# Token-major products of a two-layer hybrid backbone: one pass over the weights for two token tiles

## The chip, the cores and the metric

The kernel runs as one program on one core of a Trainium2 chip. A core has a matrix engine (TensorE, PE), a vector engine (VectorE, DVE), a scalar engine (ScalarE, ACT), GpSimd (POOL), a queue engine (SyncE, SP) that issues the DMAs, and 16 DMA engines. Matrix products are written to PSUM, which has eight banks of 512 fp32 columns on 128 partitions; everything else lies in SBUF. The metric is the device time of one execution in microseconds (us). Before the change the median of three runs is 2991.73 us (2989.30 to 2992.11).

## The reference

Two layers over 256 latent tokens and 256 context tokens of width 1024, in fp32. Each layer is a half-step SwiGLU, a parallel token mixing and a second half-step SwiGLU, all with adaptive shift, scale and gate. The token mixing starts from one wide input projection of the normalised tokens:

```
cols_x = split_cols(hx @ p['w_in'], IN_SPLITS)     # latent tokens
cols_s = split_cols(hs @ p['w_in'], IN_SPLITS)     # context tokens
# IN_SPLITS: retention q, k, v, gate; attention q, k, v; RWKV inputs; three branch gates
ret_x = retention_output(ox_f + flip_seq(ox_b), cols_x[3])
att_x = merge_att_heads(window_context_attention(aqx, akx, avx, aks, avs, sink), hx.dtype)
rwkv_x = rwkv_output(yx_f + yx_b, r_x, v_x, dirs_x, g_x, p)
out_x = branch_merge(ret_x, att_x, rwkv_x, cols_x[8], p)
```

Retention runs over 8 heads of 64 keys and 128 values, attention over 8 query and 2 key heads of 64 with a norm and a rotary step on queries and keys, RWKV-7 over 8 heads of 64 as a recurrence in both directions. In the second layer only the latent tokens have outputs; the context tokens still give keys, values and final states.

## The kernel before

Activations lie feature-major: 8 tiles of 128 features by 512 tokens (columns 0 to 255 context, 256 to 511 latent). Each such tile is held as a high and a low part (`hall`), and so is each weight, and a product takes three matmuls per slice of the contraction: high by high, high by low, low by high. That is `mm3`, lines 186 to 188, which nearly all products go through.

Weights come in one stream per stage, packed in the order of use in tiles of four 128x128 blocks (`PB = 4`, 256 KB). `Weights.get` (lines 104 to 121) hands out a block. When the tile that it lies in is not held, it issues the DMA (`raw`), an ACT copy to the high part (`whi`, L114) and a DVE subtract to the low part (`wlo`, L115), and then keeps this tile and the one just before it, no others. There are 8 buffers of `raw`, 4 of `whi` and 3 of `wlo`.

Most products (`dense`) have the weights stationary and the tokens moving, 512 or 256 columns, so that the result is feature-major. Three kinds need tokens on partitions instead: the retention values (`ret_proj`, four head pairs per layer, 256 columns each), the attention keys and values (`att_kv`, once per layer) and the attention queries (`att_q`, two groups of 256 columns per layer). There the tokens are stationary, 128 at a time, and the weights move, 256 columns. Each product covers 16 blocks: 8 slices of the contraction by two blocks side by side. In layer 0 these lie in 4 tiles; in layer 1 the stream is shifted by two blocks, and they touch 5. A half (256 tokens) is computed as two token tiles into the two halves of one bank (`ps_mm`, two buffers); the first tile's whole contraction runs before the second's:

```
for t in range(2):
    tk = slice(half * 256 + t * 128, half * 256 + t * 128 + 128)
    for kt in range(KT):
        mm3(o[:, t * 256:t * 256 + 256], hl(H[kt], tk), W.get(bl[2 * kt], 2), kt == 0, kt == KT - 1)
```

Since only two tiles are held, the walk over the weights is fetched, cast and subtracted anew for each token tile: four walks per product where both halves are wanted, two in `att_q` of layer 1. What reads the bank (a mean in `ret_proj`, the norm in `qk_norm`) reads both token tiles together.

The order of the work in the mixing stage is the string `ORDER[l]`: `P` retention projections of a head pair, `H` one retention head, `kv`, `q` and `t` attention, `c` the RWKV columns of a head pair, `A`/`C` the front steps of its context and latent halves (`rw_prep`), `B`/`D` their merge and recurrence (`rw_back`), `G` gates. From this stream a scheduler makes one fixed order of instructions for each engine, which moves an instruction past others on its engine where its own timing model finds it ready. On the chip each engine follows its order strictly. A front step ends in matmuls of L973; POOL then solves 32x32 triangles for every head and chunk (L1001, L1002), the result goes through a DRAM tile (`td`) back to SBUF (`z`), and the merge begins with stream transposes on DVE (L1016, L1020) and 32x32 matmuls on PE (L1028). The recurrence follows (L1070 to L1101).

Of the kernel before, what the change touches and what calls it, by code (L numbers as in the profile page):

```python
# [20 lines left out]
KT = 8  # L21
# [101 lines left out]
def body(nc, tc, I, O, es, dbg=None):  # L123
# [10 lines left out]
    def ps(tag):  # L134
        return pp.tile([128, 512], F32, name="ps_" + tag, tag=tag, bufs=NB[tag])
# [49 lines left out]
    def mm3(o, w, h, start, stop):  # L185
        PE.matmul(o, w[0], h[0], start=start, stop=False)  # L186
        PE.matmul(o, w[0], h[1], start=False, stop=False)  # L187
        PE.matmul(o, w[1], h[0], start=False, stop=stop)  # L188
# [138 lines left out]
    def hl(h, c):  # L327
        return h[0][:, c], h[1][:, c]
# [151 lines left out]
    def ret_decay(h, st):  # L480
# [12 lines left out]
        V.tensor_tensor(dt[1], dt[1], e, ALU.add)  # L493
        return dt

    def ret_proj(W, H, p, S, st):
        c = span(S)
        full = slice(0, 512)
        o = ps("mm")
        dense(W, f"rq{p}", H, c, o)  # L500
        q = rope_fm(o, c, st)
        o = ps("mm")
        dense(W, f"rk{p}", H, full, o)
        k = rope_fm(o, full, st)
        bl = W.take(f"rv{p}")
        v = []
        for half in range(2):
            o = ps("mm")
            for t in range(2):
                tk = slice(half * 256 + t * 128, half * 256 + t * 128 + 128)  # L510
                for kt in range(KT):
                    mm3(o[:, t * 256:t * 256 + 256], hl(H[kt], tk), W.get(bl[2 * kt], 2), kt == 0, kt == KT - 1)
            ov = o.rearrange("p (a d) -> p a d", d=128)
            mu = sm(4, "mu")
            V.tensor_reduce(mu, ov, axis=AX.X, op=ALU.add)
            V.tensor_scalar(mu, mu, -1.0 / 1024, None, ALU.mult)
            vt = ft()
            V.scalar_tensor_tensor(vt.rearrange("p (a d) -> p a d", d=128), ov, 0.125, mu.unsqueeze(2).to_broadcast([128, 4, 128]), ALU.mult, ALU.add)
            v.append(vt)
        st["ret"] = q, k, v  # L520
# [131 lines left out]
        st["aeye"] = ph[:, 0:64].bitcast(BF16)  # L652
        A.copy(st["aeye"], ident)

    def att_tok(W, H, bl, half):
        o = ps("mm")
        for t in range(2):
            tk = slice(half * 256 + t * 128, half * 256 + t * 128 + 128)
            for kt in range(KT):
                mm3(o[:, t * 256:t * 256 + 256], hl(H[kt], tk), W.get(bl[2 * kt], 2), kt == 0, kt == KT - 1)  # L660
        return o

    def qk_norm(o, nh, half, j, st):

        nc_ = nh * 64
# [37 lines left out]
    def att_kv(W, H, st):  # L703
        bl = W.take("akv")
        kt_ = ps("ap")
        vt = mk([128, 512], "kv", 1)
        for half in range(2):
            o = att_tok(W, H, bl, half)
            z = qk_norm(o, 2, half, 1, st)
            for t in range(2):  # L710
                q = half * 2 + t
                PE.transpose(kt_[:, q * 128:q * 128 + 128], z[:, t * 256:t * 256 + 128], ident)
                A.copy(vt[:, q * 128:q * 128 + 128], o[:, t * 256 + 128:t * 256 + 256])
        kd = [mk([128, 512], "kd", 2, F32R) for h in range(2)]
        kl = [mk([128, 512], "kl", 2, F32R) for h in range(2)]
        for h in range(2):
            hs, ot = (slice(64 * x, 64 * x + 64) for x in (h, 1 - h))
            A.copy(kd[h][hs], kt_[hs])
            A.copy(kd[h][ot], kt_[hs])
            V.tensor_sub(kl[h][hs], kt_[hs], kd[h][hs].bitcast(F32))  # L720
            V.tensor_sub(kl[h][ot], kt_[hs], kd[h][hs].bitcast(F32))
        st["kT"], st["v"] = (kd, kl), vt

    def att_q(W, H, grp_, S, st):
        bl = W.take(f"aq{grp_}")
        c = span(S)
        qT = [[mk([128, 512], "qT", 4, F32R) for h in range(2)] for pr in range(2)]
        for half in S:
            o = att_tok(W, H, bl, half)
            z = qk_norm(o, 4, half, 0, st)  # L730
            pt = ps("ap")
            for pr in range(2):
                for t in range(2):
                    PE.transpose(pt[:, pr * 256 + t * 128:pr * 256 + t * 128 + 128], z[:, t * 256 + pr * 128:t * 256 + pr * 128 + 128], ident)
            for pr in range(2):
                for h in range(2):
                    hs, ot = (slice(64 * x, 64 * x + 64) for x in (h, 1 - h))
                    A.copy(qT[pr][h][hs, CS[half]], pt[hs, pr * 256:pr * 256 + 256])
                    V.tensor_sub(qT[pr][h][ot, CS[half]], pt[hs, pr * 256:pr * 256 + 256], qT[pr][h][hs, CS[half]].bitcast(F32))
        st["qT", 2 * grp_], st["qT", 2 * grp_ + 1] = qT  # L740
# [474 lines left out]
    for l in range(2):  # L1215
# [5 lines left out]
        if l == 0:  # L1221
# [3 lines left out]
            H = norm(0, 0, 0, both, fine)  # L1225
            tk = tasks(0, range(2, 9))
        else:
            H = norm(1, 0, 0, both)
            ada_cond()
            tk = tasks(1, range(5, 9))  # L1230
        W = Weights(nc, mk, I[f"w{l}a"], plan_ffn("f1i", "f1o"))
# [4 lines left out]
        H = norm(l, 1, 3, both)  # L1236
# [3 lines left out]
        W = Weights(nc, mk, I[f"w{l}b"], plan_mix(l), True)  # L1240
# [114 lines left out]
```

## Time and profile before

| | |
|---|---|
| median of three runs | 2991.73 us (2989.30 to 2992.11) |
| the profiled execution | 2988.53 us, span from first to last instruction 2986.8 us |
| granted clock of TensorE, mean | 0.962 |
| PE busy | 2847.7 us (95%) |
| DVE busy | 2061.5 us (69%) |
| ACT busy | 1324.0 us (44%) |
| POOL busy | 388.8 us (13%) |
| read from HBM | 398.74 MB |

The layers' mixing stages stand at about 400 to 1330 us and 2090 to 2790 us of the span; before, between and behind them are the SwiGLU steps. A row of the views names the line, the engine, the operation and its tiles (output<-inputs) by the program's names: `ps_mm<-hall,whi` is a product with weights stationary, `ps_mm<-whi,hall` and `ps_mm<-wlo,hall` one with tokens stationary. A matmul's row lasts from its issue to its modelled end, and the rows of a running product overlap.

### The profile page before, as it was taken

How to read it: one execution, taken by the hardware profiler on the slowest of the kernel's cores; microseconds unless marked ns; L12 is line 12 of the kernel's file. 1: busy time of each engine (PE TensorE's matmuls, PEld its weight loads, DVE VectorE, ACT ScalarE, POOL GpSimd, SP SyncE). 2: the span in 40 equal slices, each digit the busy share in tenths (PEclk: the TensorE clock that was granted, in tenths of full speed). 3: DMA queues.
4: the chain of work that ended last, by engine and by line, in shares of the span. 5: the costliest groups of instructions: out<-in, count | busy, mean ns of one | idle time of the engine just before them, and what ended most of it. 6: DMA issues, size and time to landing. Idle time of an engine off the chain costs nothing.

```text
span 2986.8 us, 48345 instructions
## 1 busy us (share of the span) xinstructions
PE 2847.7 (95%) x17081; PEld 2427.4 (81%) x17081; DVE 2061.5 (69%) x4677; ACT 1324.0 (44%) x2892; POOL 388.8 (13%) x1068
## 2 busy tenths in 40 slices
PE   8999998899989999999999999999989999989999
PEld 7888887777877787788888888888778888779999
DVE  7977679785685665667756476455887778668655
ACT  3222245554454554333223332233666565655544
POOL 0000002432032121000000000000033434230000
PEclk9999999887999999999999999999989899999999
DMA  7756445332343144543544435343444344257563
GB/s 271 234 177 201 148 131 163 102 97 60 101 141 101 58 147 134 174 171 136 193 140 148 145 110 194 103 162 118 136 138 134 102 136 122 72 166 228 177 191 115
DMA packets 276434, 431.43 MB, mean 144 GB/s; under 512 B 80608, under 2 KB 98144, under 8 KB 276192
## 3 DMA queue, kind: packets, MB, share of 16 engines
q1 hardware_dynamic: 276192, 428.35, 44.8%
q8 instruction: 134, 2.20, 0.3%
q14 instruction: 108, 0.88, 0.1%
HBM read 398.74 MB, written 25.82 MB: 142 GB/s over the span
## 4 chain that ended last, share of the span: by engine, by line
PE 77%; DVE 7%; POOL 6%; DMA 4%; issue 2%; ACT 2%; SPq 1%; POOLq 0%; DVEq 0%; ACTq 0%
PE ps_mm L187 20%; PE ps_mm L188 20%; PE ps_mm L186 20%; POOL cst L1002 3%; POOL cst L1001 3%; PE ps_rf L973 2%; PE ps_mm L364 1%; DVE wlo L115 1%; PE ps_po L776 1%; DMA z<-td 1%; PE ps_po L553 1%; PE ps_rx L1077 1%; PE ps_rx L1070 1%; PE ps_rx L364 1%; PE ps_rx L1045 1%
## 5 line engine op out<-in xcount | busy, mean ns | idle before, releaser
L114 ACT CAST whi<-raw 128x512 fp32r<-128x512 f32 x1070 | 629.4, 617 | 700.3 <-PE ps_mm L187 372.7
L188 PE MATMUL ps_mm<-hall,wlo 128*128 128x512 f32 (+1 forms) x2320 | 845.0, 365 | 2.8 <-DVE wlo L115 2.7
L186 PE MATMUL ps_mm<-hall,whi 128*128 128x512 f32 (+1 forms) x2320 | 843.5, 364 | 3.5 <-ACT ft L583 2.5
L187 PE MATMUL ps_mm<-hall,whi 128*128 128x512 f32 (+1 forms) x2320 | 840.0, 362 | 0.0
L115 DVE TENSOR_TENSOR wlo<-raw,whi 128x512 fp32r<-128x512 f32 x1070 | 720.4, 690 | 87.7 <-ACT whi L114 72.9
L186 PEld LDWEIGHTS ps_mm<-hall,whi 128*128 128x128 f32 x2320 | 443.2, 191 | 74.1 <-ACT ft L583 2.7
L188 PEld LDWEIGHTS ps_mm<-hall,wlo 128*128 128x128 f32 x2320 | 442.1, 191 | 73.8 <-DVE wlo L115 4.2
L187 PEld LDWEIGHTS ps_mm<-hall,whi 128*128 128x128 f32 x2320 | 442.2, 191 | 73.3 <-issue 0.7
L186 PE MATMUL ps_mm<-hid,whi 128*128 128x512 f32 (+1 forms) x737 | 260.6, 354 | 0.0
L187 PE MATMUL ps_mm<-hid,whi 128*128 128x512 f32 (+1 forms) x737 | 260.0, 354 | 0.0
L188 PE MATMUL ps_mm<-hid,wlo 128*128 128x512 f32 (+1 forms) x737 | 257.3, 354 | 0.0
L1001 POOL TENSOR_TENSOR cst<-acc,cst 128x60 f32<-128x60 f32 (+24 forms) x496 | 176.5, 356 | 571.9 <-DMA acc<-ad__11190 55.8
L401 DVE TENSOR_TENSOR ft<-ft,ps_mm 128x512 f32<-128x512 f32 (+1 forms) x80 | 49.7, 622 | 211.4 <-PE ps_mm L188 198.3
L373 DVE SCALAR_TENSOR_TENSOR x<-ps_mm,cst,x 128x256 f32<-128x256 f32 x136 | 61.0, 480 | 192.2 <-PE ps_mm L188 192.1
L853 POOL TENSOR_TENSOR ll<-lora,lh 128x512 fp32r<-128x512 f32 x8 | 10.7, 1338 | 1396.6 <-DVE cst L199 954.4
L1002 POOL TENSOR_TENSOR cst<-cst 128x60 f32<-128x60 f32 (+24 forms) x496 | 183.0, 369 | 37.9
L236 DVE SCALAR_TENSOR_TENSOR ft<-m,cd 128x1024 bf16<-128x1024 f32 x136 | 162.8, 1219 | 7.0 <-DMA m<-ada 6.9
L237 DVE SCALAR_TENSOR_TENSOR m<-m,cd 128x1024 f32<-128x1024 f32 x136 | 165.2, 1220 | 0.7
L187 PEld LDWEIGHTS ps_mm<-hid,whi 128*128 128x128 f32 x737 | 139.0, 189 | 19.6
L186 PEld LDWEIGHTS ps_mm<-hid,whi 128*128 128x128 f32 x737 | 139.0, 189 | 19.6
L188 PEld LDWEIGHTS ps_mm<-hid,wlo 128*128 128x128 f32 x737 | 138.4, 189 | 19.2
L187 PE MATMUL ps_mm<-wlo,hall 128*128 128x256 f32 x416 | 134.0, 323 | 19.9 <-DVE wlo L115 19.1
(338 smaller groups left out, 4493.4 us busy)
## 6 DMA issues: line engine op xcount, KB each, us to landing
m<-ada SPq DMA_DIRECT2D x136, 512.0 KB, 4.5
raw<-w1b SPq DMA_DIRECT2D x271, 256.0 KB, 3.9
raw<-w0b SPq DMA_DIRECT2D x270, 256.0 KB, 3.2
raw<-w0a SPq DMA_DIRECT2D x132, 256.0 KB, 2.8
raw<-w0c SPq DMA_DIRECT2D x132, 256.0 KB, 4.8
raw<-w1a SPq DMA_DIRECT2D x132, 256.0 KB, 4.1
raw<-w1c SPq DMA_DIRECT2D x132, 256.0 KB, 3.0
gd<-ft SPq DMA_DIRECT2D x24, 256.0 KB, 2.0
```

What stands on the lines that cost most here:

```text
L114: nc.scalar.copy(hi, raw)
L115: nc.vector.tensor_sub(lo, raw, hi.bitcast(F32))
L186: PE.matmul(o, w[0], h[0], start=start, stop=False)
L187: PE.matmul(o, w[0], h[1], start=False, stop=False)
L188: PE.matmul(o, w[1], h[0], start=False, stop=stop)
L236: V.scalar_tensor_tensor(junk, raw, 1.0, st["cond"][0], ALU.mult, ALU.mult, accum_out=md[:, kt, 0:1])
L237: V.scalar_tensor_tensor(raw, raw, 1.0, st["cond"][1], ALU.mult, ALU.mult, accum_out=md[:, kt, 1:2])
L364: PE.matmul(o[:, p], w[k, j][q], hl(H[k], p)[0], start=(k == 0 and q == 0 and p.start == c.start), stop=False)
L373: V.scalar_tensor_tensor(xs[n][:, CS[s]], o[:, CS[s]], gate[:, n, s:s + 1], xs[n][:, CS[s]], ALU.mult, ALU.add)
L973: PE.matmul(ov[:, q, 0:n], kb[d][hs, q].rearrange("p a t -> p (a t)"), ar[d][hs, q].rearrange("p a t -> p (a t)")[:, 0:n], start=True, sto ...
L1001: G.tensor_tensor(w, acc[j // 16][:, j % 16, j + 1:32].unsqueeze(1).to_broadcast([128, m, n]), tt[:, 0:m, j:j + 1].to_broadcast([128, m, n ...
L1002: G.tensor_tensor(tt[:, 0:m, j + 1:32], tt[:, 0:m, j + 1:32], w, ALU.add)
```

## The change

One helper takes the place of the loop in `ret_proj` and of `att_tok`. The slices of the contraction are outside and the two token tiles inside, so a pair of weight blocks is asked for once and serves both tiles. The start flag is set for the first matmul on the bank alone, and the stop flag for the last.

```
+    def tokens(W, H, bl, half):
+
+        o = ps("mm")
+        for kt in range(KT):
+            w = W.get(bl[2 * kt], 2)
+            for t in range(2):
+                tk = slice(half * 256 + t * 128, half * 256 + t * 128 + 128)
+                mm3(o[:, t * 256:t * 256 + 256], hl(H[kt], tk), w, kt == 0 and t == 0, kt == KT - 1 and t == 1)
+        return o
+
     def ret_proj(W, H, p, S, st):
...
         for half in range(2):
-            o = ps("mm")
-            for t in range(2):
-                tk = slice(half * 256 + t * 128, half * 256 + t * 128 + 128)
-                for kt in range(KT):
-                    mm3(o[:, t * 256:t * 256 + 256], hl(H[kt], tk), W.get(bl[2 * kt], 2), kt == 0, kt == KT - 1)
+            o = tokens(W, H, bl, half)
...
-    def att_tok(W, H, bl, half):
-        o = ps("mm")
-        for t in range(2):
-            tk = slice(half * 256 + t * 128, half * 256 + t * 128 + 128)
-            for kt in range(KT):
-                mm3(o[:, t * 256:t * 256 + 256], hl(H[kt], tk), W.get(bl[2 * kt], 2), kt == 0, kt == KT - 1)
-        return o
-
...
-            o = att_tok(W, H, bl, half)
+            o = tokens(W, H, bl, half)
```

The two kernels' orders hold the same instructions but for 116 weight tiles: 116 rows of L114 on ACT, of L115 on DVE and of the `raw` DMA on SP are not in the changed one. Lines of the RWKV part have numbers lower by 2 after the change (L1028 is L1026), those of the retention heads higher by 6 (L515 is L521).

PE in the first group of token products of layer 0 (names with their numbers, so that a weight tile can be told from the next), before:

```order
L186 MATMUL ps_mm_4631<-whi_4645,hall_66 128x256
L187 MATMUL ps_mm_4631<-wlo_4646,hall_66 128x256
L188 MATMUL ps_mm_4631<-whi_4645,hall_66 128x256
L186 MATMUL ps_mm_4631<-whi_4645,hall_66 128x256
L187 MATMUL ps_mm_4631<-wlo_4646,hall_66 128x256
L188 MATMUL ps_mm_4631<-whi_4645,hall_66 128x256
L186 MATMUL ps_mm_4631<-whi_4657,hall_66 128x256
L187 MATMUL ps_mm_4631<-wlo_4658,hall_66 128x256
L188 MATMUL ps_mm_4631<-whi_4657,hall_66 128x256
```

and after the change:

```order
L186 MATMUL ps_mm_4607<-whi_4645,hall_66 128x256
L187 MATMUL ps_mm_4607<-wlo_4646,hall_66 128x256
L188 MATMUL ps_mm_4607<-whi_4645,hall_66 128x256
L186 MATMUL ps_mm_4607<-whi_4645,hall_66 128x256
L187 MATMUL ps_mm_4607<-wlo_4646,hall_66 128x256
L188 MATMUL ps_mm_4607<-whi_4645,hall_66 128x256
L186 MATMUL ps_mm_4607<-whi_4645,hall_66 128x256
L187 MATMUL ps_mm_4607<-wlo_4646,hall_66 128x256
L188 MATMUL ps_mm_4607<-whi_4645,hall_66 128x256
L186 MATMUL ps_mm_4607<-whi_4645,hall_66 128x256
L187 MATMUL ps_mm_4607<-wlo_4646,hall_66 128x256
L188 MATMUL ps_mm_4607<-whi_4645,hall_66 128x256
```

A pair of weight tiles (high and low) serves 6 matmuls before and 12 after.

DVE in the last retention-value product of layer 1, between the reading of its first half and that of its second (L515, after the change L521, is the mean over a half), before:

```order
L515 TENSOR_REDUCE cst<-ps_mm 128x4
L115 TENSOR_TENSOR wlo<-raw,whi 128x512 x2
L516 TENSOR_SCALAR cst<-cst 128x4
L115 TENSOR_TENSOR wlo<-raw,whi 128x512
L518 SCALAR_TENSOR_TENSOR ft<-ps_mm,cst 128x512
L115 TENSOR_TENSOR wlo<-raw,whi 128x512 x7
L515 TENSOR_REDUCE cst<-ps_mm 128x4
```

and after the change, from the same row on:

```order
L521 TENSOR_REDUCE cst<-ps_mm 128x4
L115 TENSOR_TENSOR wlo<-raw,whi 128x512
L537 TENSOR_TENSOR rks<-ft,rks 64x512
L1099 TENSOR_TENSOR rb<-rb,ps_rx 64x128
L1018 STREAM_TRANSPOSE tg<-z 32x8x32
L115 TENSOR_TENSOR wlo<-raw,whi 128x512
L1018 STREAM_TRANSPOSE tg<-z 32x8x32
L522 TENSOR_SCALAR cst<-cst 128x4
L980 STREAM_TRANSPOSE rt<-rt 64x256
L976 TENSOR_TENSOR gk<-ps_rf,cst 64x512
L978 TENSOR_TENSOR tg<-ps_rf,cst 64x256
L115 TENSOR_TENSOR wlo<-raw,whi 128x512
```

Ten low parts stood there and five stand now, and steps of the RWKV chain, with the transposes of the solve's result among them, have moved in between.

PE at the merge of the context half of the last head pair in layer 1, before:

```order
L186 MATMUL ps_mm<-whi,hall 128x256
L187 MATMUL ps_mm<-wlo,hall 128x256
L188 MATMUL ps_mm<-whi,hall 128x256
L186 MATMUL ps_mm<-whi,hall 128x256
L1028 MATMUL ps_rx<-rb,cst 32x32 x8
L1028 MATMUL ps_rx<-z,cst 32x32
L187 MATMUL ps_mm<-wlo,hall 128x256
```

and after the change:

```order
L186 MATMUL ps_mm<-hall,whi 128x256
L1123 MATMUL ps_rx<-cst,rb 128x64 x4
L1124 MATMUL ps_rx<-lo,cst 128x256
L1026 MATMUL ps_rx<-rb,cst 32x32 x8
L1026 MATMUL ps_rx<-z,cst 32x32 x8
L187 MATMUL ps_mm<-hall,whi 128x256
```

The merge has moved from within the last token product to a later product with the weights stationary. Between this merge and the next one, that of the latent half, stand 261 rows of PE's order before and 130 after.

## Rows read from the trace of the kernel before

**Rows 1.** The page, part 1: busy us (share of the span) xinstructions.

```profile
PE 2847.7 (95%) x17081; PEld 2427.4 (81%) x17081; DVE 2061.5 (69%) x4677; ACT 1324.0 (44%) x2892; POOL 388.8 (13%) x1068
```

**Rows 2.** Timeline of PE inside a token product: start us, us, instruction.

```profile
461.60 0.28 PE L186 MATMUL ps_mm<-whi,hall 128*128 128x256 f32 x1
461.71 0.28 PE L187 MATMUL ps_mm<-wlo,hall 128*128 128x256 f32 x1
...
462.54 0.28 PE L188 MATMUL ps_mm<-whi,hall 128*128 128x256 f32 x1
```

**Rows 3.** Groups by line: xcount | busy us, mean ns | idle before <-releasers.

```profile
L115 DVE TENSOR_TENSOR wlo<-raw,whi 128x512 fp32r<-128x512 f32 x1069 | 720.0, 691 | 87.7 <-ACT whi L114 72.9 <-PE ps_mm L188 5.7 <-POOL cst L1001 2.7
L114 ACT CAST whi<-raw 128x512 fp32r<-128x512 f32 x1069 | 629.1, 617 | 700.3 <-PE ps_mm L187 372.7 <-issue 272.7 <-PE ps_mm L188 16.6
...
L187 PE MATMUL ps_mm<-wlo,hall 128*128 128x256 f32 x416 | 134.0, 323 | 19.9 <-DVE wlo L115 19.1
L186 PE MATMUL ps_mm<-whi,hall 128*128 128x256 f32 x416 | 122.0, 296 | 2.5 <-ACT whi L114 0.9 <-DVE ft L518 0.8 <-DVE ft L572 0.7
L188 PE MATMUL ps_mm<-whi,hall 128*128 128x256 f32 x416 | 121.5, 293 | 0.0
```

**Rows 4.** Windows: us, busy of PE, PEld, DVE, ACT, POOL, clock, DMA share, GB/s.

```profile
459.00:500.00 41.00, 34.05 (x254) 30.77 (x252) 40.40 (x86) 28.08 (x59) 2.07 (x5) 1.00 0.67 207
818.00:842.00 24.00, 23.38 (x187) 21.27 (x186) 18.49 (x42) 16.84 (x42) 0.00 (x0) 1.00 0.52 169
860.00:896.00 36.00, 27.78 (x164) 23.45 (x163) 31.92 (x64) 18.86 (x41) 16.54 (x37) 0.81 0.46 131
...
2140.00:2197.00 57.00, 47.63 (x313) 41.90 (x311) 53.37 (x132) 40.99 (x88) 13.69 (x31) 0.89 0.64 210
```

**Rows 5.** Instructions on the high weight tiles: count, ns min/median/max, first and last start.

```profile
L186 PE MATMUL ps_mm<-whi,hall x416: 276/281/581, 459.6 to 2647.9; 128*128 128x256 f32 x139
```

**Rows 6.** Instructions of L187: the token products' low parts.

```profile
L187 PE MATMUL ps_mm<-wlo,hall x416: 277/282/582, 459.8 to 2648.0; 128*128 128x256 f32 x139
```

**Rows 7.** The page, part 6: DMA issues, count, KB each, us to landing.

```profile
raw<-w1b SPq DMA_DIRECT2D x271, 256.0 KB, 3.9
raw<-w0b SPq DMA_DIRECT2D x270, 256.0 KB, 3.2
```

**Rows 8.** Groups by line, 818 to 842 us: the second query group of layer 0.

```profile
L187 PE MATMUL ps_mm<-wlo,hall 128*128 128x256 f32 x32 | 9.8, 306 | 0.0
L186 PE MATMUL ps_mm<-whi,hall 128*128 128x256 f32 x32 | 9.1, 289 | 0.0
L188 PE MATMUL ps_mm<-whi,hall 128*128 128x256 f32 x32 | 9.0, 281 | 0.0
```

**Rows 9.** Timeline of DVE at 885 us; in brackets idle before and releaser.

```profile
885.53 0.43 DVE L1020 STREAM_TRANSPOSE tg<-z 32x256 f32<-32x256 f32 x1 [2.52 <-DMA z<-td]
885.90 0.64 DVE L115 TENSOR_TENSOR wlo<-raw,whi 128x512 fp32r<-128x512 f32 x1
```

**Rows 10.** Timeline of PE at 886 us.

```profile
886.59 0.58 PE L187 MATMUL ps_mm<-wlo,hall 128*128 128x256 f32 x1 [2.79 <-DVE wlo L115]
```

**Rows 11.** Waits of the whole span: us in total, times, longest.

```profile
DVE tg L1020 <- DMA z<-td: 37.0, 15, 5.7
```

**Rows 12.** Timeline of PE at the merges of layer 1's last head pair.

```profile
2627.67 0.59 PE L1028 MATMUL ps_rx<-rb,cst 32*32 32x32 f32 x13
...
2680.63 0.87 PE L1028 MATMUL ps_rx<-rb,cst 32*32 32x32 f32 x13 [1.03 <-DVE cst L1093]
```

**Rows 13.** Groups by line, 860 to 896 us: the third retention group of layer 0.

```profile
L187 PE MATMUL ps_mm<-wlo,hall 128*128 128x256 f32 x32 | 12.1, 378 | 6.7 <-DVE wlo L115 6.6
L188 PE MATMUL ps_mm<-whi,hall 128*128 128x256 f32 x32 | 10.6, 331 | 0.0
L186 PE MATMUL ps_mm<-whi,hall 128*128 128x256 f32 x32 | 10.6, 331 | 0.0
```

More of the change, by code (lines that the diff above doesn't have):

```diff
@@ L728, in att_q @@
         for half in S:
-            o = att_tok(W, H, bl, half)
+            o = tokens(W, H, bl, half)
             z = qk_norm(o, 4, half, 0, st)
```

## The prediction, made before the changed kernel was run

> **What bounds the kernel now.** I read the page first, then the groups of instructions by line with shapes kept apart, then the windows of the token products, and last the timelines inside them.
>
> The page shows TensorE (PE) busy for 95% of the span and VectorE (DVE) for 69% [rows 1]. PE's share flatters it, because a matmul's row holds its whole passage: inside an undisturbed token product a row lasts 0.28 us, but 8 starts (461.60 to 462.54) take 0.94 us, 0.1175 each [rows 2]. So the reader should look at starts and at stretched durations, not at busy time. One token product of 128 tokens by 256 columns ("pass") is 8 slices of the contraction by 3 matmuls, 24 starts, 2.82 us of PE. Its weights are 4 tiles of 128x512, and each of them costs DVE 691 ns (the low part) and ScalarE (ACT) 617 ns (the high part) [rows 3]: 2.76 us of DVE and 2.47 us of ACT for 2.82 us of PE. An uninterrupted token product thus leaves DVE almost no time, and DVE also carries rotary, norm and RWKV work. There are 416/8 = 52 passes [rows 3].
>
> The windows show what follows: in 459 to 500 us DVE is busy 40.4 of 41.0 us, in 2140 to 2197 it is busy 53.4 of 57.0, in 860 to 896 it is busy 31.9 of 36.0, and PE is busy 34.1, 47.6 and 27.8 us there [rows 4]. The low part ends these waits: of PE's idle time before the token matmuls, 19.1 of 22.4 us are put down to it [rows 3].
>
> **How large the stall is.** Two parts, both from the groups of the whole span [rows 3].
> Idle time of PE in front of the three matmul lines: 19.9 + 2.5 + 0.0 = 22.4 us.
> Stretched rows: the undisturbed median is 281 ns on L186 and 282 on L187 [rows 5, 6]; I use 281 for L188 too. The means are 323, 296 and 293 [rows 3], so L187 is 41, L186 15 and L188 12 ns too long: 68 ns x 416 = 28.3 us.
> Together 50.7 us of the span of 2986.8.
>
> **What the change removes.** The weights are now asked for once per half (256 tokens) instead of once per 128 tokens. The order of the changed program has 116 weight tiles fewer: 56 in layer 0 (270 fetches become 214) and 60 in layer 1 (271 become 211) [rows 7]. Per tile: one DMA of 256 KB, one ACT cast, one DVE subtract. So 116 x 0.691 = 80.2 us of DVE, 116 x 0.617 = 71.6 us of ACT, 30 MB of traffic and 116 issues of SP go. The matmuls, their shapes and their number stay, so no PE work is removed: the gain can only be waiting.
>
> The supply now has room: a tile serves 12 matmuls (1.41 us) where it served 6 (0.705 us), against 0.691 us of DVE. What waiting remains? The nearest rows are those of a group of four passes (the second query group of layer 0) whose weights came almost in time: in 818 to 842 us four passes took 24 us because other work lay between them, DVE was at 18.5 of 24 us and the clock was full [rows 4]. There PE had no idle time before the token matmuls, and the means were 306, 289 and 281 ns [rows 8]: 24 + 8 + 0 = 32 ns on 32 matmuls of each line, 1.0 us for four passes. For 52 passes that leaves 13 x 1.02 = 13.3 us. So 50.7 - 13.3 = 37.4 us go. The bounds of this term are 0 (everything is given back later) and 50.7 (nothing remains), and I take 37.4, since even an uninterrupted group will ask for 4 tiles in 5.64 us, 0.71 per us, about the 0.67 per us (16 in 24 us) of that row.
>
> **What it adds and moves.** The second token tile's matmuls stand between the first's, in one bank. The bank was already held until both tiles were done, because the readers (mean, norm) read the whole tile, so nothing behind the bank is later; 0 us, or at most one pass (2.82 us) once per group of either kind if a reader could have started after the first tile, which the kernel before doesn't do either. A weight tile is held twice as long: its buffers (4 high, 3 low, 8 raw) turn over half as fast, and fewer are needed; 0 us.
>
> Small work of other chains that the scheduler had put into the waits of a token product now stands behind more of it. The order shows this for the merges of the triangular solve (the 32x32 matmuls of L1028, L1026 after the change): in layer 1 the merge of the last head pair's context half stood inside the last token product and now stands behind it, in a product whose weights are stationary. And on DVE the transposes of the solve's result (L1020, now L1018) stand between the low parts of that last token product. Such a neighbour has a price in the trace: at 882 us DVE waited 2.52 us for the solve's result to land, the low part stood behind it, and PE then waited 2.79 us for that low part [rows 9, 10]. Over the kernel DVE waited 37.0 us in 15 places at this transpose [rows 11]. On the other side, 80 us less of DVE work shortens the queue in front of every small DVE step of a chain. I have no row for either sum; from nothing to 37.0 us lost on the one side, from nothing to 80.2 - 37.4 = 42.8 us gained on the other. The two ends are nearly equal, so I enter 0 and keep both for the range.
>
> **The sum.** The profiled execution took 2988.5 us: its span of 2986.8 and 1.7 around it. 2988.5 - 37.4 = 2951.1. The median of the runs, 2991.7, is 3.2 us above the profiled one, so the forecast is 2954 us, 1.3% faster.
>
> **Rivals.**
> *DVE was the real bound of the whole mixing stage.* Then more than the token stalls go: at the end all 80.2 us that DVE loses, 2911 us. For it: DVE's share in the windows above. Against it: outside the token groups, PE idles for ACT, DMA and its own small matmuls as well. Halfway between (37.4 + 21.4 = 58.8 us) gives 2933.
>
> *The wait moves to the solve.* PE reaches the merges earlier, but the solve's result lands when it lands (front step, chain of POOL operations, two DMAs). If all 16 merges were waited for, the whole gain would be given back there: 2991.7, or about 2980 if a third of it stays. For it: the waits at the transposes [rows 9, 11]. Against it: at 2627.67 PE entered a merge without idle time, and at 2680.63 it waited 1.03 us, for DVE [rows 12], so the merges are not all late.
>
> *Slower: the recurrence of layer 1's last head pair loses its cover.* The merges of its context and latent halves stood 53.0 us apart (2627.67 and 2680.63) [rows 12] with 261 rows of PE's order between them; now 130 rows stand there. If the 53.0 us are the recurrence's own latency and not the rows' work, 131/261 of them, 26.6 us, become waiting; with the gain given back at the earlier merges as well, 2991.7 + 26.6 = 3018 us. It decides from the point where the recurrence takes longer than the 130 rows do. Against it: the recurrence interleaves with other rows throughout, and what follows the last half is dense work that doesn't need its result at once.
>
> *Slower: the inner loop no longer runs one output tile's contraction through.* With the weights outside, PE may have to wait at each slice, and its clock falls. In 860 to 896 us, where a pass waited longest, the granted clock was 0.81 on average, with 1.00 in 818 to 842 [rows 4]; the means there were 378, 331 and 331 ns and PE idled 6.7 us before L187 [rows 13]. If every four passes cost as much, 96 + 50 + 50 = 196 ns x 32 = 6.3 us and 6.7 us idle, 13 x 13.0 = 169 us stand where 50.7 did: 3110 us. Against it: the order before ran each contraction through and fell to this state all the same; the state follows the missing weights.
> The Trainium skill, in TensorE: Matmul & The Clock Gate, section "HAM oscillation — how this bites in real kernels", advises to run all slices of the contraction for one output tile before waiting for data, so that the clock stays up; the new order does the opposite. By that rule this rival would win; the trace doesn't bear it out, since the window with 0.81 had the advised order.
>
> That the change doesn't remove the fetches is excluded by the order's 116 rows.
>
> **How the numbers follow.** Forecast with 37 us (2942 to 2972): 0.55. DVE relief beyond it (2911 to 2942): 0.17. Gain given back for the most part (2972 to 2992): 0.18. Recurrence uncovered (up to 3018): 0.08. Clock lost (3110): 0.02. The range of 8 in 10 leaves out the fastest part of the relief and the slower cases: 2922 to 2988. A measurement of this kernel can tell 0.2%, 6 us, from no change. Faster by more than that: 0.55 + 0.17 + half of 0.18, 0.81; within it the other half, 0.09; slower 0.10.
>
> **What would show it right or wrong.** Right: the three token groups have means near 281 to 306 ns and almost no idle time; DVE's busy time falls by 80 us and ACT's by 72; the clock in layer 0's third retention group (860 to 896 us here) and in layer 1's first token groups is near 1.00; no new wait of PE at the merges. Wrong in the step of the stall: idle time before the token matmuls stays above 10 us. Wrong in the step of the neighbours: token groups clean, but DVE's and ACT's waits for the solve's result, or PE's before the recurrence's matmuls, grow by tens of us; the span then moves by less than the stall that went. Wrong the other way: waits of PE for small DVE steps outside the token groups shrink by 20 us or more.

## The result, and the profile after

The changed kernel takes 2952.67 us (median of four runs, 2949.03 to 2961.04) against 2990.52 us for the one before in the same runs (2984.36 to 2992.11). The ratio is 0.9885, with a 95% interval of 0.9867 to 0.9904: 1.15% faster. The forecast was 2954. The profiled execution took 2949.03 us, its span 2947.2, 39.6 us less than the span before.

The page after, part 1, in the columns of [rows 1]:

```profile
PE 2821.4 (96%) x17081; PEld 2413.6 (82%) x17081; DVE 1991.8 (68%) x4561; ACT 1261.4 (43%) x2776; POOL 372.5 (13%) x1068
```

DVE lost 69.7 us and ACT 62.6 against [rows 1]. The groups by line, to be read against [rows 3]:

```profile
L115 DVE TENSOR_TENSOR wlo<-raw,whi 128x512 fp32r<-128x512 f32 x953 | 645.4, 690 | 229.6 <-issue 106.8 <-ACT whi L114 61.8 <-PE ps_mm L188 28.0
...
L114 ACT CAST whi<-raw 128x512 fp32r<-128x512 f32 x953 | 568.0, 617 | 653.7 <-PE ps_mm L187 429.7 <-issue 125.6 <-PE ps_mm L188 34.0
...
L187 PE MATMUL ps_mm<-wlo,hall 128*128 128x256 f32 x416 | 123.7, 297 | 2.6 <-DVE wlo L115 2.4
L186 PE MATMUL ps_mm<-whi,hall 128*128 128x256 f32 x416 | 122.3, 295 | 2.3 <-DVE ft L524 1.3 <-ACT whi L114 1.0
L188 PE MATMUL ps_mm<-whi,hall 128*128 128x256 f32 x416 | 121.7, 293 | 0.0
```

116 casts and 116 subtracts are gone. PE's idle time before the token products fell from 22.4 us to 4.9, and the share of it that the low part ended from 19.1 to 2.4. The relation has turned: DVE's idle time in front of a low part, 87.7 us before, is now 229.6, and 28.0 of it waits for PE to give a buffer back, where 5.7 did.

The first token groups of layer 0, the groups of P1 and P2 (second and third retention pair) and the first two of layer 1, as windows in the columns of [rows 4]:

```profile
461.70:490.00 28.30, 27.34 (x227) 26.68 (x226) 27.49 (x71) 17.36 (x35) 2.07 (x5) 1.00 0.51 152
627.00:650.00 23.00, 23.00 (x186) 20.63 (x185) 16.69 (x36) 13.75 (x35) 10.50 (x30) 1.00 0.43 121
836.00:858.00 22.00, 20.27 (x150) 19.12 (x149) 17.15 (x37) 11.75 (x28) 9.71 (x26) 0.84 0.51 140
2122.70:2167.00 44.30, 41.65 (x311) 39.85 (x310) 36.16 (x99) 27.77 (x64) 4.75 (x10) 0.92 0.48 142
```

The token products of 459 to 500 us before stand in 28.3 us now, the third retention group in 22 where it took 36, layer 1's first groups in 44.3 where they took 57. Not all of that is gain. In the windows of layer 0's first groups and of the third retention group fewer other matmuls stand between the token products than before (35 where 62 did, 54 where 68 did); in layer 1's it is much the same (119 and 121).

The span divides by stage as follows; a boundary is the first matmul of a stage's first product. The mixing stage of layer 0 went from 927.2 to 905.7 us, that of layer 1 from 700.3 to 678.4, and all the rest grew by some 4 us in sum.

**A second measure of the token products.** A matmul's row is 0.28 us long where matmuls start every 0.1175 us [rows 2], so a wait shorter than the row's tail leaves no idle time in the view. I therefore also walked PE's matmuls in their order, charged each with the time from the end of the one before to its own end, and added these up over the two mixing stages. For the token products this gives 204.0 us before and 168.0 after (1248 matmuls at 0.1175 would be 146.6); for all other matmuls of these stages 1424.7 and 1417.9. The idle time in front of a stage's first matmul counts with the stage here, and by this account the rest of the program grew by 3.2 us: 36.0 + 6.8 - 3.2 is the 39.6 us of the span. Of the 36.0 us, 30.6 lie in three places: the first groups of layer 0 (29.8 to 22.9 us), the third retention group (24.9 to 14.1) and the first groups of layer 1 (39.5 to 26.8). "Token sum" and "other sum" below are the two sums; each comes from one profiled execution.

### The profile page after: what moved, and what is told of

The parts are those of the page before. It is cut to its first block, busy times and chain, and to the rows that moved or that the text cites. A ratio compares the mean times of both kernels' runs of the same rounds, so it can differ in the third digit from the quotient of the medians.

```text
span 2947.2 us, 47745 instructions
## 1 busy us (share of the span) xinstructions
PE 2821.4 (96%) x17081; PEld 2413.6 (82%) x17081; DVE 1991.8 (68%) x4561; ACT 1261.4 (43%) x2776; POOL 372.5 (13%) x1068
## 4 chain that ended last, share of the span: by engine, by line
PE 79%; POOL 7%; DVE 5%; DMA 4%; issue 2%; ACT 2%; SPq 1%; POOLq 0%; DVEq 0%; ACTq 0%
PE ps_mm L186 21%; PE ps_mm L187 20%; PE ps_mm L188 20%; POOL cst L1000 3%; POOL cst L999 3%; PE ps_rf L971 2%; PE ps_mm L364 1%; PE ps_po L774 1%; PE ps_rx L1075 1%; PE ps_rx L1068 1%; PE ps_rx L364 1%; PE ps_po L559 1%; DMA z<-td 1%; DVE wlo L115 1%; DMA td<-cst 1%
## 5 line engine op out<-in xcount | busy, mean ns | idle before, releaser
L114 ACT CAST whi<-raw 128x512 fp32r<-128x512 f32 x954 | 568.4, 617 | 655.1 <-PE ps_mm L187 429.7
L187 PE MATMUL ps_mm<-hall,whi 128*128 128x512 f32 (+1 forms) x2320 | 839.0, 362 | 0.0
L115 DVE TENSOR_TENSOR wlo<-raw,whi 128x512 fp32r<-128x512 f32 x954 | 645.8, 689 | 230.0 <-issue 106.8
L187 PEld LDWEIGHTS ps_mm<-hall,whi 128*128 128x128 f32 x2320 | 440.6, 190 | 70.5 <-issue 0.3
L187 PE MATMUL ps_mm<-hid,whi 128*128 128x512 f32 (+1 forms) x737 | 259.9, 354 | 0.0
L1000 POOL TENSOR_TENSOR cst<-cst 128x60 f32<-128x60 f32 (+24 forms) x496 | 172.7, 348 | 37.8
L373 DVE SCALAR_TENSOR_TENSOR x<-ps_mm,cst,x 128x256 f32<-128x256 f32 x136 | 61.0, 480 | 146.6 <-PE ps_mm L188 146.3
L187 PEld LDWEIGHTS ps_mm<-hid,whi 128*128 128x128 f32 x737 | 139.1, 189 | 19.5
L210 ACT CAST hid<-ft 128x512 fp32r<-128x512 f32 (+1 forms) x88 | 49.9, 568 | 192.5 <-DVE ft L401 192.4
```

The source lines that it names most:

```text
L114: nc.scalar.copy(hi, raw)
L115: nc.vector.tensor_sub(lo, raw, hi.bitcast(F32))
L373: V.scalar_tensor_tensor(xs[n][:, CS[s]], o[:, CS[s]], gate[:, n, s:s + 1], xs[n][:, CS[s]], ALU.mult, ALU.add)
L1000: G.tensor_tensor(tt[:, 0:m, j + 1:32], tt[:, 0:m, j + 1:32], w, ALU.add)
```

## The experiments

Times are medians, each ratio is against the kernel before in the same runs. "Stall" is the prediction's measure: PE's idle time before the three token lines, plus the mean length of their rows over 281, 282 and 281 ns, times 416.

| kernel | time, us | ratio (95%) | stall | token sum | other sum |
|---|---|---|---|---|---|
| before (profiled run 2988.5) | 2990.5 | 1 | 50.7 | 204.0 | 1424.7 |
| after | 2952.7 | 0.9885 (0.9867 to 0.9904) | 22.0 | 168.0 | 1417.9 |
| e1 DMA, ACT, DVE twice | 2994.4 | 1.0010 (0.9992 to 1.0028) | 45.1 | 194.2 | 1435.8 |
| e2 DVE twice | 2962.9 | 0.9903 (0.9884 to 0.9922) | 45.2 | 195.5 | 1401.6 |
| e3 ACT twice | 2974.8 | 0.9948 (0.9932 to 0.9965) | 22.6 | 168.5 | 1440.7 |
| e4 DMA twice | 2972.2 | 0.9937 (0.9919 to 0.9955) | 31.3 | 175.9 | 1435.5 |
| e5 before, low part last | 3020.5 | 1.0108 (1.0093 to 1.0124) | 51.7 | 205.7 | 1454.1 |
| e6 after, low part last | 2967.2 | 0.9924 (0.9909 to 0.9938) | 20.2 | 165.7 | 1436.0 |
| e7 zigzag | 2977.2 | 0.9961 (0.9946 to 0.9976) | 28.1 | 178.4 | 1433.6 |
| e8 five tiles held | 2962.4 | 0.9912 (0.9898 to 0.9927) | 17.5 | 165.2 | 1442.0 |
| e9 before, high by low first | 3017.2 | 1.0073 (1.0054 to 1.0092) | 62.6 | 212.7 | 1439.4 |
| e10 after, high by low first | 2987.0 | 0.9983 (0.9969 to 0.9997) | 23.1 | 169.0 | 1453.4 |
| e11 retention only | 3009.5 | 1.0056 (1.0037 to 1.0075) | 41.3 | 189.3 | 1449.4 |
| e12 attention only | 3002.2 | 1.0028 (1.0014 to 1.0042) | 47.9 | 196.0 | 1449.4 |

The two sums don't move together. Everything that follows rests on keeping them apart.

**e1 to e4: what of a weight tile is waited for.** The changed loop, with the work on each token weight tile done twice (109 tiles): all of it, or one kind. The subtract a second time:

```
+            if again:
+                nc.vector.tensor_sub(lo, raw, hi.bitcast(F32))
...
-            w = W.get(bl[2 * kt], 2)
+            w = W.get(bl[2 * kt], 2, True)
```

e3 repeats `nc.scalar.copy(hi, raw)` in the same way, e4 the DMA into a further `raw` buffer that nothing reads, and e1 all three.

> The changed loop, but each weight tile asked for by a token product costs one more DMA into an unread buffer, one more ACT cast and one more DVE subtract, so the weight work is that of the kernel before (1063 casts and subtracts, 109 of the 116 removed), in the new loop order. Theory (the gain is the weight work that went, 116 tiles): the time goes back to about 2988 us (2980 to 2994), and idle time plus stretch of the token matmuls goes back from 22 us to about 50. Rival (the new order of loops or the scheduler's new order made the gain): about 2953 us, token matmuls as after the change.

> As e1, but only the DVE subtract is done twice (1063 subtracts, casts and DMAs as after the change). Theory (the low part on DVE is what the token products waited for): most of the way back, 2980 us (2972 to 2990), DVE busy back by 75 us, the idle time before L187 put down to DVE's low part back above 12 us. Rival (ACT casts or DMA traffic mattered as much): 2960 us or less. Rival (order): 2953.

> As e1, but only the ACT cast is done twice (1063 casts). Theory (DVE is the limit, ACT has room at 43% busy): 2955 us (2948 to 2962), although 67 us of ACT work come back. Rival (every engine's weight work counts): 2965 us or more. Rival (order): 2953.

> As e1, but only the DMA is issued twice, into an unread buffer (535 fetches in the mixing stages, 109 more). Theory: 2954 us (2948 to 2960), since the DMA share is below 0.7 in the token windows and raw tiles land ahead. Rival (traffic was part of the stall): 2965 us or more, with the ACT casts of the token products waiting for raw.

The groups by line of e2, with the added subtract:

```profile
L189 PE MATMUL ps_mm<-wlo,hall 128*128 128x256 f32 x416 | 125.1, 301 | 19.7 <-DVE wlo L117 19.7
L190 PE MATMUL ps_mm<-whi,hall 128*128 128x256 f32 x416 | 121.7, 293 | 0.0
L188 PE MATMUL ps_mm<-whi,hall 128*128 128x256 f32 x416 | 121.0, 293 | 7.6 <-DVE rr_v L801 6.9 <-DVE ft L580 0.7
...
L117 DVE TENSOR_TENSOR wlo<-raw,whi 128x512 fp32r<-128x512 f32 x109 | 75.1, 694 | 1.5
```

of e3, with the added cast:

```profile
L188 PE MATMUL ps_mm<-whi,hall 128*128 128x256 f32 x416 | 123.4, 297 | 4.4 <-DVE rr_k L801 2.2 <-DVE ft L526 2.2
L189 PE MATMUL ps_mm<-wlo,hall 128*128 128x256 f32 x416 | 123.3, 296 | 1.1 <-DVE wlo L117 1.1
...
L116 ACT CAST whi<-raw 128x512 fp32r<-128x512 f32 x109 | 66.7, 618 | 1.9
```

and of e4, with the added DMA:

```profile
L190 PE MATMUL ps_mm<-wlo,hall 128*128 128x256 f32 x416 | 124.7, 300 | 8.4 <-DVE wlo L118 8.4
```

75.1 us of DVE work put back bring 27.5 us of the token sum back (168.0 to 195.5), and the wait for the low part with them, 19.7 us where [rows 3] have 19.1. 66.7 us of ACT work bring 0.5 us, 109 transfers of 256 KB 7.9. So the wait of the kernel before was for the most part one for DVE, with a smaller part that comes with the transfers; e4 doesn't tell their traffic from the `raw` buffers that they take. The casts cost the token products nothing. All three together bring 26.2, no more than DVE alone: the terms don't add. And with nearly all of the weight work back (109 tiles of 116), 9.8 of the 36.0 us of gain stay. No run here tells whether the new loop spreads the same work better or the order does it.

The times missed what I expected, but for e1, which was expected at 2988 and came at 2994. e2 was expected at 2980 and came at 2963, e3 and e4 at 2955 and 2954 and came at 2975 and 2972, where their rivals had put them (2965 or more). The token sums went as the theory said, but for e4's, and the other sums went by -16, +23 and +18 us from that of after (1417.9), for e2, e3 and e4. For e3 the rows don't show the casts themselves as the cause of the +23: from after to e3, PE's idle time in front of the other matmuls rose where DVE ended it (45.8 to 68.3 us), and DVE has no work added; where ACT ended it, it fell (44.6 to 32.8). A repeated instruction changes what the scheduler sees, and it makes another order everywhere: of PE's 14963 places, 1753 (e4) to 5409 (e2) hold another instruction than in the changed kernel. For comparison, 5402 differ between before and after.

**e5, e6, e9, e10: the same change under other orders.** To see what an order alone is worth, both loops were run with the three matmuls of a token product in another sequence. Work and weight tiles are those of before and of after. e5 and e6 take the low weights last:

```
+    def mm3t(o, w, h, start, stop):
+        PE.matmul(o, w[0], h[0], start=start, stop=False)
+        PE.matmul(o, w[1], h[0], start=False, stop=False)
+        PE.matmul(o, w[0], h[1], start=False, stop=stop)
```

(arguments are given so that tokens are `w` here), and e9 and e10 start with `w[0], h[1]`, the low weights.

> The kernel before, with one thing neutral to the weight work: in token products the matmul with the weights' low part comes third of the three instead of second. The scheduler makes another order of it (5141 of 14963 places on PE hold another instruction). This measures what a new order is worth by itself, beside 0.1 us more time for each low part. Theory (weight work decides, the order of small work is worth little): 2989 us (2982 to 2995). Rival (the order of small work is worth as much as the change): anywhere from 2955 to 3020, more than 12 us from 2991.

> The changed kernel with the same neutral step (low part third; 3718 places on PE hold another instruction). Theory: 2952 us (2944 to 2960), so that e6 less e5 is 38 us give or take 10. Rival (order): the difference between e5 and e6 is not the change's 38 us but anything between 10 and 70.

> A third matched pair, before: in token products the matmul with the weights' low part comes first of the three (4147 places on PE hold another instruction than in the kernel before). Theory now (two terms: the token products' waiting, fixed by the weight work; and what the scheduler's order makes of the small work, worth 15 us either way and not tied to the change): token matmuls as before, 50 us of idle time and stretch together (45 to 56); the time 2990 us give or take 20. Rival (the change as such also makes better orders): see e10.

> The changed kernel with the same neutral step (4154 places on PE hold another instruction). Theory: token matmuls' idle time and stretch together 22 us (18 to 28), so that pair e9 to e10 gains about 36 us by the token products, with 15 to 20 us of scatter from the order: time 2945 to 2980, below e9 by 15 to 60. Rival (the gain of 38 us is mostly luck of the order): e10 not below e9 by more than 10 us.

The low weights' row of e5 and, in the next fence, that of e6:

```profile
L193 PE MATMUL ps_mm<-wlo,hall 128*128 128x256 f32 x416 | 132.1, 320 | 22.4 <-DVE wlo L115 22.0
```

```profile
L193 PE MATMUL ps_mm<-wlo,hall 128*128 128x256 f32 x416 | 123.1, 296 | 0.3 <-DVE wlo L115 0.3
```

and of e9 and e10:

```profile
L191 PE MATMUL ps_mm<-wlo,hall 128*128 128x256 f32 x416 | 136.5, 328 | 29.7 <-DVE wlo L115 28.7 <-DVE ft L577 0.6
```

```profile
L191 PE MATMUL ps_mm<-wlo,hall 128*128 128x256 f32 x416 | 124.1, 298 | 8.1 <-DVE wlo L115 3.2 <-DVE ft L529 2.9 <-DVE rr_v L804 2.0
```

e9's stall of 62.6 us is above the 45 to 56 that I expected, e10's 23.1 within 18 to 28. All four times came out longer than I expected: e5 at 3020.5 for 2989, e6 at 2967.2 for 2952, e9 at 3017.2 for 2990 give or take 20, e10 at 2987.0 for 2945 to 2980. So the theory of e5, that the order of small work is worth little, was wrong; the differences e6 less e5 (-53.3, expected 38 give or take 10) and e10 less e9 (-30.2, expected 15 to 60) have the sign of the change. These three pairs are the cleanest test of the change. From the old loop to the new one:

| pair | time | token sum | other sum |
|---|---|---|---|
| before to after | -37.9 | -36.0 | -6.8 |
| e5 to e6 | -53.3 | -40.0 | -18.1 |
| e9 to e10 | -30.2 | -43.7 | +14.0 |
| mean | -40.5 | -39.9 | -3.6 |

The token sum falls by 36 to 44 us in each. The other sum goes either way, and its mean is near nothing. Within one loop, the order alone makes up to 30 and 34 us: before, e5 and e9 run at 2990.5, 3020.5 and 3017.2 us, after, e6 and e10 at 2952.7, 2967.2 and 2987.0. Each kernel of this case has the best order of its three, so neither is favoured against the other.

**e7, e8: fewer weight tiles by other means.** Both keep the old loop, the first tile's whole contraction before the second's. e7 walks the second one backwards and so finds the last two tiles held (57 tiles fewer than before):

```
-                for kt in range(KT):
-                    mm3(..., W.get(bl[2 * kt], 2), kt == 0, kt == KT - 1)
+                for i in range(KT):
+                    kt = KT - 1 - i if t else i
+                    mm3(..., W.get(bl[2 * kt], 2), i == 0, i == KT - 1)
```

e8 holds all tiles of a product for both halves, in five buffers each of `whi` and `wlo` (169 tiles fewer):

```
-            s.cur = {q: v for q, v in s.cur.items() if q == p - 1}
+            s.cur = {q: v for q, v in s.cur.items() if q == p - 1 or hold is not None and q >= hold}
```

> The kernel before with its loop order kept (a token tile's whole contraction first), but the second token tile of a half walks the slices backwards, so that the two tiles still held serve again: 57 weight tiles fewer instead of 116. Theory (the gain goes with the tiles removed, whatever the loop order): about half, 2972 us (2962 to 2982). Rival (the loop order makes the gain): 2990 us. Rival (the token stall needs the low part to come at half the rate at every tile): under a quarter of the gain, 2983 us or more.

> The kernel before with its loop order, but all weight tiles of a token product are held until its end (5 high and 5 low buffers instead of 4 and 3): 169 tiles fewer, 53 more than the change removes. Theory (gain by tiles removed, and what is left of the stall after the change is small): 2940 us (2928 to 2955). Rival (the stall is all that counts, and 22 of 51 us are left): 2950 us. Rival (five buffers bound to one product keep the next product's weights from being made ready): 2960 us or more.

The low weights' row of e7, then that of e8:

```profile
L187 PE MATMUL ps_mm<-wlo,hall 128*128 128x256 f32 x416 | 126.3, 305 | 9.5 <-DVE wlo L115 9.4
```

```profile
L187 PE MATMUL ps_mm<-wlo,hall 128*128 128x256 f32 x416 | 120.0, 289 | 1.4 <-DVE wlo L115 1.4
```

Half of the tiles saved takes 25.6 us off the token sum of before, 169 saved take 38.8. So the gain follows the tiles and doesn't need the new inner loop: the old order reaches the same token sum where its weights are held. Beyond the 116 tiles hardly anything is left to gain; e8 has 53 fewer than after, a token sum 2.8 us lower, an other sum 24 us higher, and takes 9.8 us longer. e7's time is within what I expected (2962 to 2982). e8's is not (2928 to 2955); it lies where the rival of the bound buffers had it (2960 or more). But PE's idle time for weights outside the token products is 1.9 us there and 1.0 after, while that for the recurrence's `rb` tiles is 37.3 and 18.1, so the rows point to the order and not to the buffers.

**e11, e12: the change in one place only.** e11 takes the new loop in `ret_proj` alone (72 tiles fewer than before), e12 in `att_kv` and `att_q` alone (44 fewer). In each the other place keeps the loop of before:

```
-            o = tokens(W, H, bl, half)
+            o = att_tok(W, H, bl, half)
```

> The new loop for the retention values alone (32 of 52 passes, 72 of 116 tiles); attention as before. Theory: idle time and stretch of the token matmuls from 51 to about 30 us, since the groups that waited longest before (860 to 896 and 2140 to 2165 us) are retention's; the token term gains about 24 us, the time 2966 us give or take 15. Rival (the tiles removed count wherever they are): 72/116 of 38, 2967 us, but with the token term spread evenly (51 to 33).

> The new loop for attention's keys, values and queries alone (20 of 52 passes, 44 of 116 tiles). Theory: idle time and stretch from 51 to about 40 us, the time 2979 us give or take 15; the token terms of e11 and e12 add up to that of the whole change within 6 us, the times need not, because each has its own order. Rival (times add up): e11 and e12 together gain 38 us within 5.

The low weights' row of e11, then that of e12:

```profile
L187 PE MATMUL ps_mm<-wlo,hall 128*128 128x256 f32 x416 | 127.4, 306 | 20.1 <-DVE wlo L115 20.0
```

```profile
L187 PE MATMUL ps_mm<-wlo,hall 128*128 128x256 f32 x416 | 132.6, 319 | 14.3 <-DVE wlo L115 14.0
```

Each part lowers the token sum, by 14.7 and 8.0 us, roughly in the proportion of their tiles. That is less than I expected: the stall was to be about 30 and 40 and measures 41.3 and 47.9, and the two parts were to add up to the whole within 6 us and give 22.7 of the 36.0. And both kernels, expected at 2966 and 2979 us, are slower than before (3009.5 and 3002.2), since their other sums are 24.7 us higher. Against before alone one would call either part harmful. Against the mean of the three kernels with the old loop, (2990.5 + 3020.5 + 3017.2)/3 = 3009.4, e12 is 7.2 us faster and e11 equal, which is inside what an order makes. Whether the two parts need each other or merely met poor orders was not settled: a pair under other orders for each would have been needed.

**Where an order's 20 us lie.** PE's idle time before all matmuls but the token ones, in the two mixing stages, adds up to 89.7 us before, 94.1 after, 102.7 in e5, 98.3 in e9 and 114 in e11 and e12. A place that recurs is the end of a head pair's recurrence, where PE transposes the normed output. The waits of e12 (us in total, times, longest) have 16.7 us there:

```profile
PE ps_rx L1127 <- DVE rb L1124: 16.7, 5, 5.2
```

In the kernel before, instructions on the tile `rb` and PE's waits for it:

```profile
L1125 PE MATMUL ps_rx<-cst,rb x48: 216/223/366, 618.4 to 2733.3; 64*128 64x64 f32 x48
...
  DVE rb L1122: 1.7, 3
```

and in the kernel after:

```profile
L1123 PE MATMUL ps_rx<-cst,rb x48: 222/223/337, 607.3 to 2708.3; 64*128 64x64 f32 x48
...
  DVE rb L1120: 12.1, 5
```

with the row of the last of them, on PE's timeline:

```profile
2708.07 0.46 PE L1123 MATMUL ps_rx<-cst,rb 64*128 64x64 f32 x4 [3.40 <-DVE rb L1120]
```

PE's order is fixed, and so it stands at these transposes until DVE has normed the rows; 1.7 us have become 12.1. The rest of the difference between the other sums (for e5, 29.4 us over before, of which only 13.0 are idle time) lies in the rows, stretched or held up for less than a row's tail. One part of that is the clock: its mean over the whole run is 0.953 in e5 and 0.954 in e9 against 0.962 before. How much the clock makes of it was not worked out. Why one order has more of such places than another was not traced further.

## Why the prediction was right

**The stall and its cause: right.** The low part of the weights was what PE waited for: its 19.1 us are 2.4 now, and DVE's work alone, put back (e2), brings them again, with 27.5 of the 36.0 us.

**The size: 37.4 us forecast, 36.0 by the token sum.** By the prediction's own measure 28.7 of the 50.7 us went, since 22.0 remain where it left 13.3. That step, taken from one group of four passes [rows 8], was too low by 8.7 us. Of the 22.0, 4.9 us are idle time and 17.1 stretch, and about two thirds of the stretch (11.5 us) is in the 84 token matmuls that ran at half the clock (below), where that group had it in full. The measure itself sees too little, because short waits hide below a row's tail; the two misses cancel. Over the three pairs the mean is 39.9 us.

**The neighbours: 0 entered, a gain of 3.6 us measured, but not for the reason given.** The other sum fell by 6.8 us and the rest of the program rose by 3.2. That the two ends cancel was a guess, and the pairs show a spread of -18 to +14 around it. The wait at the solve's result, one of the two ends, hardly moved: of the waits after, against the 37.0 us of [rows 11],

```profile
DVE tg L1018 <- DMA z<-td: 35.1, 10, 5.1
```

A loss that did come stands elsewhere, at the output of the recurrence (1.7 to 12.1 us). The relief showed too: outside the token products PE's idle time ended by DVE fell from 57.9 to 45.8 us, less than the 20 that were to prove the forecast too small, and that ended by ACT rose from 27.0 to 44.6. The chance of 0.10 for slower and the range of 2922 to 2988 were of the right width: e6 and e10, the same work under other orders, lie at 2967 and 2987.

**The sum.** 2954 forecast, 2952.7 measured. So close a hit holds luck: that of the order, since the same change is worth 30 to 53 us in the three pairs, and that of the two misses in the size.

**The removed work: right in its count, small in its price.** 116 tiles, as the order said; the page's DMA issues against [rows 7]:

```profile
raw<-w0b SPq DMA_DIRECT2D x214, 256.0 KB, 2.9
raw<-w1b SPq DMA_DIRECT2D x211, 256.0 KB, 3.0
```

DVE's busy time fell by 69.7 us rather than 80, ACT's by 62.6 rather than 72. The lines of the weights alone fell by 74.6 and 61.1 us (720.0 to 645.4, 629.1 to 568.0), so DVE's other work takes some 5 us more in its rows.

**The clock: wrong.** It was to be near 1.00 in the third retention group and in layer 1's first groups. It went from 0.81 to 0.84 and from 0.89 to 0.92 (windows above, [rows 4]). The prediction said that the fall follows the missing weights, and that with the weights in time it would not come. In the third group the rows put no idle time of PE down to the low part now, and the clock falls all the same. Windows of the kernel after show where:

```profile
845.00:850.00 5.00, 3.31 (x28) 2.66 (x27) 3.90 (x10) 3.45 (x10) 3.04 (x9) 0.91 0.36 98
850.00:855.00 5.00, 4.96 (x26) 4.66 (x25) 4.01 (x9) 1.14 (x2) 4.22 (x10) 0.50 0.76 235
```

and PE's timeline there what stood ahead of it:

```profile
844.65 0.28 PE L188 MATMUL ps_mm<-whi,hall 128*128 128x256 f32 x1
...
847.63 0.49 PE L1079 MATMUL ps_rx<-ve,kbT 128*128 128x128 f32 x2 [0.61 <-ACT ve L1077]
848.49 0.49 PE L1079 MATMUL ps_rx<-ve,kbT 128*128 128x128 f32 x2 [0.38 <-ACT ve L1077]
849.69 1.30 PE L1096 MATMUL ps_rx<-ve,tg 64*64 64x64 f32 x8 [0.71 <-DVE cst L1091]
851.02 0.58 PE L187 MATMUL ps_mm<-wlo,hall 128*128 128x256 f32 x1
...
851.62 0.41 PE L186 MATMUL ps_mm<-whi,hall 128*128 128x256 f32 x1
851.83 0.41 PE L187 MATMUL ps_mm<-wlo,hall 128*128 128x256 f32 x1
```

Inside a token product, between the first matmul on a new weight tile and the first on its low part, stand steps of the recurrence, of which three wait for ACT or DVE; PE is busy 3.31 of 5 us, the clock is granted at half in the next 5, and the token matmuls that follow start every 0.21 us rather than every 0.1175. But this low part was late. DVE's timeline has no low part between these two rows,

```profile
840.30 0.69 DVE L115 TENSOR_TENSOR wlo<-raw,whi 128x512 fp32r<-128x512 f32 x1
...
850.28 2.07 DVE L115 TENSOR_TENSOR wlo<-raw,whi 128x512 fp32r<-128x512 f32 x3
```

and the first of the three, which is the one that the product goes on with, ended at 850.97 us, 0.05 us before it did. The small steps stand in that wait, so this group neither proves nor refutes that the fall follows the weights. Layer 1 does refute it. The first three low parts for the second half of attention's keys and values were done by 2147.60 us, that product began at 2157.43, behind small steps again, and ran at half the clock, one matmul every 0.21 us:

```profile
2146.28 1.32 DVE L115 TENSOR_TENSOR wlo<-raw,whi 128x512 fp32r<-128x512 f32 x2
...
2155.47 0.39 PE L548 MATMUL ps_sc<-rqh,rks 128*128 128x256 f32 x1 [0.78 <-DVE rks L537]
...
2157.43 0.58 PE L186 MATMUL ps_mm<-whi,hall 128*128 128x256 f32 x1
...
2158.02 0.41 PE L188 MATMUL ps_mm<-whi,hall 128*128 128x256 f32 x1
2158.23 0.41 PE L186 MATMUL ps_mm<-whi,hall 128*128 128x256 f32 x1
```

So the half clock comes without late weights too. Still, part of the gain lies there: by end-to-end times the token matmuls at half the clock took 32.7 us before (104 of them) and 18.6 after (84).

**The rivals.** DVE as bound of the whole stage (2911 to 2942): no; DVE lost 69.7 us and the other sum 6.8, and in e2 DVE does 75.1 us more than in after while the other sum is 16.3 us lower. The solve: no, as shown. The recurrence of the last pair uncovered: no; the merges now stand 35.7 us apart, and PE entered both without idle time, on its timeline:

```profile
2608.17 0.59 PE L1026 MATMUL ps_rx<-rb,cst 32*32 32x32 f32 x13
...
2643.86 0.90 PE L1026 MATMUL ps_rx<-rb,cst 32*32 32x32 f32 x13
```

The 53.0 us of [rows 12] were for the most part the rows' own work. The prediction's ratio of 130 to 261 rows misleads, because a row there can hold many matmuls: counted singly the traces have 388 from the one merge to the next before and 271 after (0.70), and the time went with them (0.67). The inner loop's clock: no; the mean granted clock is 0.961 to 0.965 in the four runs after, 0.962 in the profiled run before, and e8 has the old order of the contraction with nearly the token sum of the new one.
The Trainium skill, in TensorE: Matmul & The Clock Gate, section "HAM oscillation — how this bites in real kernels", speaks for a whole contraction of one output tile at a time. These runs don't show that price here: the token sum is 168.0 us with the new order, 165.2 in e8 with the advised one and 53 tiles fewer.

## What to carry to other kernels

Before a loop over weights, compare the preparation of a tile per use (here 691 ns of DVE) with the matmul time that it serves (0.705 us before, 1.41 after): where they are nearly equal, other work on that engine can become waiting, and a second use of the tile while it is held removed most of it here. Where a scheduler orders the program anew at each edit, give both kernels the same neutral edit, twice or more, and compare pairs: a single variant against the kernel before (e3, e11, e12) can have the wrong size or the wrong sign. And split the span into the products that the change touches and all the rest, since the first repeated within 3 to 9 us here under three orders and the second within 29 to 36.

## What the runs showed of the hardware that was not expected

Idle time in the rows is no full measure of waiting on PE: with rows of 0.28 us that start every 0.1175 us, the rows give 28.7 us of gain where the ends of the matmuls give 36.0. And the half clock came not only where weights were late, but also behind small matmuls of which some waited for DVE (0.17 and 0.78 us in 2153 to 2156 us, with the weights ready), at the expense of the large product behind them.
